# Which chunks of weights get their low parts from an accumulating DMA: fewer of them in four stages of a decoder trunk, and 18 feed-forward pairs by blocks

## The chip, the cores and the metric

The kernel runs on one core of one Trainium2 chip. The metric is the device time of one execution in microseconds (us). A profile is one further execution, recorded by the hardware profiler; it has a time of its own, and its span runs from the first to the last instruction. Engines are named as the profile names them: PE (TensorE's matmuls), PEld (its weight loads), DVE (VectorE), ACT (ScalarE), POOL (GpSimd) and SP (SyncE, which here issues transfers).

## The reference

Two layers over 512 tokens of width 1024, in float32. Cut to what matters here:

```python
for l in range(DEPTH):                                   # DEPTH = 2
    mod = c_act @ w_ada[l] + b_ada[l]                    # 6 x 1024 modulations
    sh1, sc1, g1, sh2, sc2, g2 = jnp.split(mod, 6, axis=-1)
    h = modulate(rmsnorm(x, norm1[l]), sh1, sc1)
    q, k, v, g_sw, p_in, gates = jnp.split(h @ w_in[l], IN_SPLITS, axis=-1)
    ...                                                  # rotary, chunked retention of 8 heads, pooling
    ret_d = (jax.nn.silu(g_sw) * ret) @ w_ret_o[l]
    pool_d = (pooled * pool_scale[l]) @ w_pool_o[l]
    a_ret, a_pool = jnp.split(gates, 2, axis=-1)
    merged = jax.nn.sigmoid(a_ret) * ret_d + jax.nn.sigmoid(a_pool) * pool_d
    x = x + g1[:, None, :] * (merged @ w_out[l])
    h2 = modulate(rmsnorm(x, norm2[l]), sh2, sc2)
    gate, up = jnp.split(h2 @ w_ffn_in[l], 2, axis=-1)   # 2 x 2816 columns
    x = x + g2[:, None, :] * ((jax.nn.silu(gate) * up) @ w_ffn_out[l])
return rmsnorm(x, final_norm)
```

## The kernel before, in words

**Numbers in two parts.** PE multiplies a shorter float format (float32r). To keep float32 accuracy, each operand is split into a high part, which is its float32r rounding, and a low part, which is the rest. A product is then three matmuls: high by high, low by high, high by low (`mm3`).

**Weights in chunks.** All weight blocks of 128 x 128 are packed on the host, in the order of use, into chunks of 8 blocks (128 x 1024, 512 KB). A layer takes 131 chunks. Within a layer, chunks 0 to 27 hold q, k, v, the output gate and the pooling input; 28 to 43 the sigmoid gate of the retention branch and its output projection in turn; 44 to 56 the pooling branch; 57 to 64 the output projection; 65 to 130 the feed-forward part. The gate and up projections come in 22 pairs of column tiles, two chunks each: pairs 0 to 10 are chunks 65 to 86, then 11 chunks of the down projection (87 to 97), then pairs 11 to 21 (98 to 119), then the rest of the down projection (120 to 130).

**Preparing a chunk.** `prep` loads a chunk into one of 3 `raw` tiles (a transfer on SP's queue) and writes the high part into one of 11 `w` tiles (`copy`, on DVE or ACT). The low part, in another `w` tile, is made in one of two ways. The local way subtracts the high part from the raw tile (`nc.either`: DVE or POOL). The added way lets ACT write the negated high part and lets a transfer issued by POOL read the same chunk again from memory and add it in (`accum_op=ALU.add`). Before the change every chunk from number 16 on takes the added way. An added chunk needs its raw tile only for the cast; a local chunk needs it until the subtraction has read it.

**Pairs by blocks.** Some pairs (the set `SEVEN`) are computed as four 2 x 2 blocks by a scheme of seven products, `seven`: 84 matmuls of 256 columns for a pair, where an ordinary pair takes 48 of 512. `seven_prep` loads the chunk, forms sums of blocks on DVE, and needs four `w` tiles for it. Before the change layer 0 has 9 such pairs (4, 6, ... 20) and layer 1 has 12 (two of every three from 4 on).

**Looking ahead.** `ahead` prepares the chunk in use and the next `LOOK` = 2. A chunk is known to belong to a pair by blocks only when that pair is reached, and by then `prep` has been called for it as for an ordinary chunk. Those chunks are loaded and prepared twice, and the first result is read by nothing.

**Modulations in the background.** `mod_tile` loads 512 KB of the modulation weights into a `raw` tile and reduces it on DVE. `background` issues the next one: two after each step of the two gate loops, one after each ordinary pair and after each step of the first down projection.

**The order of work.** All operations are recorded first. A planner (`Recorder`) gives each a due time, which it derives backwards from PE's order, then simulates the engines with a cost table and lists the instructions; each engine then works its list in that order. `LANDS` is the time that the planner allows for an accumulating transfer to land. Every instruction is emitted by one line, L409, so the profile's groups are told apart by tile names: `raw` and `w` as above, `h` the normalised input, `x` pair tiles (in the feed-forward part the sums of blocks), `r` rows kept in float32r, `t` temporaries, `ps` the PSUM banks.

Of the kernel before, what the change touches and what calls it, by code (L numbers as in the profile page):

```python
# [8 lines left out]
F32 = mybir.dt.float32  # L9
F32R = mybir.dt.float32r  # L10
AF = mybir.ActivationFunctionType
ALU = mybir.AluOpType
# [14 lines left out]
FT = FF // P  # L27
# [11 lines left out]
N_UNITS = DEPTH * (44 * KT + 8 * KT + 4 + 8 * 4 + 8 * KT + 2 * FT * KT + 8 * FT)  # L39
N_CHUNKS = -(-N_UNITS // UNITS) + DEPTH  # L40
LOOK = 2
ADD_SEVEN = False
FIRST_ADDED = 16


N_RAW, N_W, N_X, N_H, N_ROW, N_TEMP = 3, 11, 8, 2 * KT, 28, 9
# [4 lines left out]
STAT_TILES = {"out": 4, "ffn_out": 3}  # L51
STAT_AT = 2

SEVEN = [set(range(4, FT, 2)), {i for i in range(3, FT) if i % 3}]
HALF_KT = KT // 2


# [143 lines left out]

TABLES = (AF.Sigmoid, AF.Silu, AF.Abs_reciprocal_sqrt)
TABLE_US = 1.28
LANDS = 5.0
LATENCY = {"tensor": 0.19, "vector": 0.05, "scalar": 0.05, "gpsimd": 0.05, "sync": 1.6}


class Recorder:
# [32 lines left out]
    def deadlines(self):  # L241
# [13 lines left out]
        for op in reversed(self.ops):  # L255
# [3 lines left out]
            for o in op.after + reuse.get(op, []):  # L259
                if o.n > op.n:  # L260
                    op.due = min(op.due, o.due - LATENCY[e] - op.cost(e) - (LANDS if op.added else 0.0))
            if op.urgent and (e == "sync" or op.table is AF.Silu):
                op.due = op.n - 1e6

    def order(self):
# [48 lines left out]
        while len(out) < len(self.ops):  # L314
# [50 lines left out]
            if e == "scalar" and o.table is not None:  # L365
                end += TABLE_US * (o.table != table)
                table = o.table
            lands = LANDS if e == "gpsimd" and o.forms[e][0] == "dma_start" else 0.0
            if e == "tensor":
# [51 lines left out]
def trunk(ctx, tc, xT, cin, wada, vecs, wst, rot, trid, icnt, out):  # L421


    nc = Recorder()
# [5 lines left out]
    def ps():  # L430
        return nc.tile(pp, [P, S], F32, "ps", 8)

    def temp():
        return padded()[:, PAD:]
# [4 lines left out]
    def keep(dt=F32R):  # L439
        return nc.tile(ap, [P, S], dt, "r", N_ROW)  # L440

    def weights():
        return nc.tile(wp, [P, UNITS * P], F32R, "w", N_W)

    def raw_tile():
        return nc.tile(wp, [P, UNITS * P], F32, "raw", N_RAW)
# [45 lines left out]
    def prep(c, n=1):  # L492
        if c >= N_CHUNKS or c in his or c in sevens:
            return
        raw, hi, lo = raw_tile(), weights(), weights()
        nc.sync.dma_start(out=raw, in_=wst[c])
        if FIRST_ADDED <= c:

            copy(hi, raw)
            nc.scalar.activation(lo, hi.bitcast(F32), AF.Copy, scale=-1.0)  # L500
            nc.gpsimd.dma_start(out=lo, in_=wst[c], accum_op=ALU.add)
        else:
            w = UNITS * P // n
            for s_ in (slice(i * w, i * w + w) for i in range(n)):
                copy(hi[:, s_], raw[:, s_])
                nc.either.tensor_sub(out=lo[:, s_], in0=raw[:, s_], in1=hi[:, s_].bitcast(F32))
        his[c], los[c] = hi, lo
# [13 lines left out]
    def seven_prep(c):  # L521

        if sevens[c] is not None:
            return
        w = 2 * P
        af = raw_tile()
        nc.sync.dma_start(out=af, in_=wst[c])
        ah, al, sh, sl = (weights() for _ in range(4))
        a11, a12, a22, a21 = (af[:, n * w:n * w + w] for n in range(4))
        s34, s21 = keep(F32), keep(F32)  # L530
        nc.vector.tensor_sub(out=s34[:, :w], in0=a21, in1=a11)
        nc.vector.tensor_add(out=s21[:, :w], in0=s34[:, :w], in1=a22)
        nc.vector.tensor_add(out=s21[:, w:], in0=a21, in1=a22)
        nc.vector.tensor_sub(out=s34[:, w:], in0=a12, in1=s21[:, :w])
        copy(ah[:, :3 * w], af[:, :3 * w])
        if ADD_SEVEN:
            nc.scalar.activation(al[:, :3 * w], ah[:, :3 * w].bitcast(F32), AF.Copy, scale=-1.0)
            nc.gpsimd.dma_start(out=al[:, :3 * w], in_=wst[c][:, :3 * w], accum_op=ALU.add)
        else:
            nc.either.tensor_sub(out=al[:, :3 * w], in0=af[:, :3 * w], in1=ah[:, :3 * w].bitcast(F32))  # L540
        for n, sf in enumerate((s34, s21)):
            part = slice(n * S, n * S + S)
            copy(sh[:, part], sf)
            nc.either.tensor_sub(out=sl[:, part], in0=sf, in1=sh[:, part].bitcast(F32))
        sevens[c] = (ah, al), (sh, sl)
# [11 lines left out]
    def ahead(c):  # L557
        for cc in range(c, c + look[0] + 1):
            if cc in sevens:
                seven_prep(cc)  # L560
            else:
                prep(cc)
# [7 lines left out]
    def copy(out, src):  # L570
        nc.add({"scalar": ("copy", (), dict(out=out, in_=src)), "vector": ("tensor_copy", (), dict(out=out, in_=src))})
# [10 lines left out]
    def project(o, l, name, col, src, sl=FULL, k0=0, mid=None):  # L582
        n = len(src)
        for k in range(n):
            if mid and k == n // 2:
                mid()
            mm3(o[:, sl], unit(l, name, k0 + k, col), hs(src[k], sl), k == 0, k == n - 1)
# [13 lines left out]
    def mod_tile(l, t):  # L601

        w = raw_tile()
        nc.sync.dma_start(out=w, in_=wada[l, t])
        nc.vector.scalar_tensor_tensor(
            out=w, in0=w, scalar=1.0, in1=cact, op0=ALU.mult, op1=ALU.mult, accum_out=mods[l][:, t:t + 1],
        )
# [18 lines left out]
    def background(n=1):  # L626
        for _ in range(n):
            if waiting:
                mod_tile(*waiting.pop(0))
# [129 lines left out]
    def start(cols):  # L759

        ss = first_norm()
        o = [ps() for _ in cols]
        for k in range(KT):
            mod_tile(0, 8 + k)
            mod_tile(0, k)
            mod_bias(0, k, 1)
            mod_bias(0, 8 + k, 1)
            gain(0, 1, k, 1)
            prep(k, 2 if k == 0 else 1)
            for sl in (A, B) if k == 0 else (FULL,):  # L770
                if k == 0:
                    rstd(rs[:, sl], dict(ss)[sl], D)
                make_h(0, 1, k, sl, h[k])
            nc.urgent = False
            if k + 1 == KT:
                look[0] = LOOK
            for sl in (A, B) if k == 0 else (FULL,):
                for n, (a, b) in enumerate(((0, 0), (1, 0), (0, 1))):
                    for t, c in zip(o, cols):
                        nc.tensor.matmul(t[:, sl], lhsT=unit(0, "in", k, c)[a], rhs=h[k][b][:, sl],  # L780
                                         start=k + n == 0 and sl.start != S // 2, stop=k + n == KT + 1)
        nc.sync.dma_start(out=ic, in_=icnt)
        nc.sync.dma_start(out=tri, in_=trid)
        return dict(zip(cols, o))
# [65 lines left out]
    for l in range(DEPTH):  # L850
# [18 lines left out]
        def filler(mid=None):  # L869

            kind, n = fill.pop(0)
            if kind == "gate":
                gate(n)
            else:
                p0[n] = pool_in(tile_of(C_P + n * P, mid))
                pd[n] = pool_diff(n, p0.pop(n))
# [10 lines left out]
        for g in range(2):  # L887
# [33 lines left out]
            for i in range(4):  # L921
# [4 lines left out]
                for j in range(4):  # L926
                    c0 = min(j, 2) * P
                    w = S - c0
# [43 lines left out]
        for j in range(KT):  # L972
            o = ps()
            project(o, l, "in", C_A + j * P, h, mid=head_norm)
            sg = temp()
            nc.scalar.activation(sg, o, AF.Sigmoid)
            while fill:
                filler()
            rp = ps()
            project(rp, l, "ret_o", j * P, y)  # L980
            m = keep(F32)
            nc.vector.tensor_mul(out=m, in0=rp, in1=sg)
            m_.append(m)
            background(2)


        merged = []
# [85 lines left out]
        for f, (i0, i1) in enumerate(zip(FF_CUTS, FF_CUTS[1:])):  # L1073
            hid = []
            for i in range(i0, i1):
                if i in SEVEN[l]:
                    hid.append(seven(i))
# [114 lines left out]
```

## Time and profile before

| what | value |
|---|---|
| three runs | 1628.1 us median (1627.85 to 1629.76) |
| profiled execution, its own time | 1639.41 us |
| its span | 1637.6 us |
| PE busy | 1536.2 us (94%) |
| DVE, ACT, POOL busy | 980.3, 700.5, 337.1 us (60%, 43%, 21%) |
| mean granted clock of PE | 0.969 of full speed |
| transfers | 353.94 MB, 216 GB/s over the span |

A busy time is the union of an engine's instructions; a matmul that waits inside a stream shows as idle time ahead of the next one. PEclk is the clock granted to PE as a share of full speed. In a group's row the count stands behind an x, then the busy time, the mean duration of one in ns, and the idle time of the engine just before them with what ended it.

### The profile page before, as it was taken

The page shows a single profiled execution, that of the slowest core. Times are in us where ns is not written, and L with a number is a line of the kernel's source. Part 1 is how long each engine was busy: PE and PEld are TensorE (multiplying, and loading weights), DVE is VectorE, ACT ScalarE, POOL GpSimd, SP SyncE. Part 2 cuts the span into 40 slices and gives each one's busy share as a digit, 9 for nine tenths or more (in the row PEclk, how much of TensorE's full clock was granted, in tenths as well). Part 3 has the DMA queues.
Part 4 walks back from the last instruction along what each step waited for, and adds up shares of the span by engine and source line. Part 5 has one row for each costly group of instructions (what it writes and reads, how often), then busy time and mean ns, then how long its engine had stood idle before and what let it go on. Part 6 is the DMA issues. An engine that isn't in the chain of part 4 may idle for free.

```text
span 1637.6 us, 21319 instructions
## 1 busy us (share of the span) xinstructions
PE 1536.2 (94%) x8058; PEld 1314.2 (80%) x8058; DVE 980.3 (60%) x1748; ACT 700.5 (43%) x983; POOL 337.1 (21%) x370
## 2 busy tenths in 40 slices
PE   7999999799998899889999999999999899987897
PEld 6788878587987778788898887887888788887787
DVE  7887663455675645575266757535537784366733
ACT  2477542323553322333257766213237543244432
POOL 0033231121132111112111322211213322122211
PEclk9999999899999999899999999999999999999999
DMA  7758779999679799979977866999978789788893
GB/s 240 267 145 216 153 193 256 267 253 270 146 220 239 212 260 243 241 218 251 250 172 170 210 155 151 260 263 276 266 158 208 183 234 259 178 210 219 223 220 89
DMA packets 101225, 353.94 MB, mean 216 GB/s; under 512 B 11265, under 2 KB 13569, under 8 KB 101122
## 3 DMA queue, kind: packets, MB, share of 16 engines
q0 software_dynamic: 35568, 129.51, 42.9%
q1 hardware_dynamic: 65554, 223.07, 39.5%
q8 instruction: 63, 1.03, 0.2%
q14 instruction: 40, 0.33, 0.1%
HBM read 350.44 MB, written 2.10 MB: 215 GB/s over the span
## 4 chain that ended last, share of the span: by engine, by line
PE 43%; DMA 33%; DVE 11%; issue 8%; ACT 3%; POOL 1%; DVEq 0%; SPq 0%; ACTq 0%; POOLq 0%
PE ps L409 43%; DMA raw<-wada 13%; DMA w<-wst 10%; DMA raw<-wst 9%; DVE w L409 4%; DVE t L409 3%; ACT w L409 2%; DVE raw L409 2%; DVE r L409 1%; POOL w L409 1%; ACT t L409 1%; DMA xall<-xT 0%; POOL r L409 0%; DVE x L409 0%; DVE h L409 0%
## 5 line engine op out<-in xcount | busy, mean ns | idle before, releaser
L409 PE MATMUL ps<-h,w 128*128 128x512 f32 (+1 forms) x3828 | 791.9, 365 | 59.1 <-DMA w<-wst 51.3
L409 PEld LDWEIGHTS ps<-h,w 128*128 128x128 f32 x3828 | 655.9, 194 | 178.7 <-DMA w<-wst 56.0
L409 PE MATMUL ps<-r,w 128*128 128x512 f32 (+1 forms) x2430 | 484.5, 359 | 19.9 <-DVE r L409 17.6
L409 PEld LDWEIGHTS ps<-r,w 128*128 128x128 f32 x2430 | 405.1, 189 | 93.0 <-DVE r L409 20.9
L409 ACT ACTIVATE w<-w 128x1024 fp32r<-128x1024 f32 x247 | 260.3, 1058 | 426.3 <-DVE w L409 158.1
L409 POOL DMA_DIRECT2D w<-wst x247 | 220.3, 895 | 1052.4 <-ACT w L409 909.2
L409 DVE CAST w<-raw 128x1024 fp32r<-128x1024 f32 (+2 forms) x202 | 140.1, 693 | 200.7 <-DMA raw<-wst 134.1
L409 DVE SCALAR_TENSOR_TENSOR raw<-raw,cact 128x1024 f32<-128x1024 f32 x96 | 120.5, 1258 | 166.8 <-DMA raw<-wada 163.1
L409 ACT CAST w<-raw 128x1024 fp32r<-128x1024 f32 (+2 forms) x104 | 103.6, 997 | 161.8 <-DMA raw<-wst 126.7
L409 PE MATMUL ps<-x,w 128*128 128x256 f32 x1008 | 125.1, 279 | 1.0 <-ACT t L409 1.0
L409 PEld LDWEIGHTS ps<-x,w 128*128 128x128 f32 x1008 | 121.1, 188 | 1.2 <-ACT t L409 1.2
L409 PE MATMUL ps<-w,h 128*128 128x512 f32 x384 | 90.2, 395 | 0.0
L409 PEld LDWEIGHTS ps<-w,h 128*128 128x128 f32 x384 | 72.1, 188 | 17.5
L409 DVE TENSOR_TENSOR w<-raw,w 128x768 fp32r<-128x768 f32 (+2 forms) x55 | 64.4, 1172 | 24.7 <-DMA w<-wst 12.2
L409 DVE SCALAR_TENSOR_TENSOR xall<-ps,mod,xall 128x512 f32<-128x512 f32 (+1 forms) x62 | 38.8, 628 | 65.7 <-PE ps L409 65.6
L409 ACT CAST r<-t 128x512 fp32r<-128x512 f32 (+1 forms) x97 | 59.6, 617 | 34.4 <-DVE t L409 27.0
L409 DVE TENSOR_TENSOR w<-r,w 128x512 fp32r<-128x512 f32 x81 | 54.4, 688 | 24.8 <-ACT w L409 16.1
L409 DVE TENSOR_TENSOR t<-ps,t 128x512 f32<-128x512 f32 x81 | 55.3, 683 | 15.3 <-PE ps L409 13.2
L409 ACT CAST w<-r 128x512 fp32r<-128x512 f32 x55 | 32.5, 617 | 71.9 <-DVE r L409 40.7
L409 DVE TENSOR_TENSOR r<-raw 128x256 f32<-128x256 f32 x84 | 41.3, 514 | 35.1 <-DMA raw<-wst 34.9
L409 DVE TENSOR_TENSOR r<-t,r 128x512 fp32r<-128x512 f32 (+1 forms) x78 | 56.7, 727 | 7.4 <-ACT r L409 6.2
L409 ACT COPY t<-ps 32x512 f32<-32x512 f32 (+2 forms) x93 | 48.8, 527 | 18.9 <-DVE t L409 11.2
(95 smaller groups left out, 1005.1 us busy)
## 6 DMA issues: line engine op xcount, KB each, us to landing
raw<-wst SPq DMA_DIRECT2D x305, 512.0 KB, 5.9
w<-wst POOLq DMA_DIRECT2D x247, 512.0 KB, 8.3
raw<-wada SPq DMA_DIRECT2D x96, 512.0 KB, 5.7
x<-rot SPq DMA_DIRECT2D x32, 256.0 KB, 7.3
xall<-xT SPq DMA_DIRECT2D x4, 512.0 KB, 6.8
out<-t SPq DMA_DIRECT2D x7, 256.0 KB, 2.3
out<-t SPq DMA_DIRECT2D x2, 128.0 KB, 1.8
tri<-trid SPq DMA_DIRECT2D x1, 128.0 KB
```

The lines of the kernel that those rows point to most:

```text
L409: getattr(eng, method)(*[real(a) for a in args], **{k: real(v) for k, v in kw.items()})
```

## The change

The flag for all chunks from 16 on becomes a function of the chunk's place in its layer. Chunks 0 to 27 (in layer 0 from 16 on, as before) and 57 to 74 keep the added way. In chunks 28 to 56 (gates), 87 to 97 and 120 to 130 (the down projection, called the output stage in the change) only even numbers keep it. In chunks 75 to 86 and 98 to 119 (pairs 5 to 10 and 11 to 21) none does. Layer 1 now has the same 9 pairs by blocks as layer 0, 18 in all in place of 21. The loop over the first gate issues one modulation a step in place of two; those left over are issued by later calls of `background`. The planner's `LANDS` goes from 5.0 to 6.0. An unused flag and its branch in `seven_prep` are gone.

```diff
-ADD_SEVEN = False
 FIRST_ADDED = 16
+LAYER_CHUNKS = 131
+
+HALF_ADDED, NONE_ADDED = ((28, 57), (87, 98), (120, 131)), ((75, 87), (98, 120))
+
+
+def is_added(c):
+
+    n = c % LAYER_CHUNKS
+    if c < FIRST_ADDED or any(a <= n < b for a, b in NONE_ADDED):
+        return False
+    return n % 2 == 0 or not any(a <= n < b for a, b in HALF_ADDED)
...
-SEVEN = [set(range(4, FT, 2)), {i for i in range(3, FT) if i % 3}]
+SEVEN = [set(range(4, FT, 2)), set(range(4, FT, 2))]
...
-LANDS = 5.0
+LANDS = 6.0
...
-        if FIRST_ADDED <= c:
+        if is_added(c):
 
             copy(hi, raw)
             nc.scalar.activation(lo, hi.bitcast(F32), AF.Copy, scale=-1.0)
...
-        if ADD_SEVEN:
-            nc.scalar.activation(al[:, :3 * w], ah[:, :3 * w].bitcast(F32), AF.Copy, scale=-1.0)
-            nc.gpsimd.dma_start(out=al[:, :3 * w], in_=wst[c][:, :3 * w], accum_op=ALU.add)
-        else:
-            nc.either.tensor_sub(out=al[:, :3 * w], in0=af[:, :3 * w], in1=ah[:, :3 * w].bitcast(F32))
+        nc.either.tensor_sub(out=al[:, :3 * w], in0=af[:, :3 * w], in1=ah[:, :3 * w].bitcast(F32))
...
             m_.append(m)
-            background(2)
+            background()
```

## The prediction

> **What bounds the kernel now.** I read the page first: transfers and instruction groups.
>
> ```profile
> span 1637.6 us, 21319 instructions
> PE 1536.2 (94%) x8058; PEld 1314.2 (80%) x8058; DVE 980.3 (60%) x1748; ACT 700.5 (43%) x983; POOL 337.1 (21%) x370
> q0 software_dynamic: 35568, 129.51, 42.9%
> q1 hardware_dynamic: 65554, 223.07, 39.5%
> raw<-wst SPq DMA_DIRECT2D x305, 512.0 KB, 5.9
> w<-wst POOLq DMA_DIRECT2D x247, 512.0 KB, 8.3
> raw<-wada SPq DMA_DIRECT2D x96, 512.0 KB, 5.7
> ```
>
> PE is nearly full, so a saving must come from its idle 101 us or its clock. The two queues are not alike: the accumulating one takes 42.9% of the span, 702.5 us, for 247 chunks, so 2.84 us of all sixteen engines each. The plain one takes 646.9 us for 223.07 MB, so 1.52 us for a chunk of 0.524 MB. And 305 plain loads are 263 chunks plus 42: the chunks of all 21 pairs by blocks are loaded twice, and 247 = 263 - 16 says that the useless copies get accumulating transfers too.
>
> Next, PE's waits, then its timeline at some of them. A timeline row gives start, length, matmuls, and in brackets the idle time ahead.
>
> ```profile
> PE ps L409 <- DMA w<-wst: 53.5, 15, 8.8
> PE ps L409 <- DVE r L409: 18.0, 6, 8.5
> ...
> 247.29 5.66 PE L409 MATMUL ps<-h,w 128*128 128x512 f32 x24
> 252.79 5.66 PE L409 MATMUL ps<-r,w 128*128 128x512 f32 x24
> 312.06 3.35 PE L409 MATMUL ps<-r,w 128*128 128x512 f32 x7 [8.52 <-DVE r L409]
> ...
> 686.98 15.25 PE L409 MATMUL ps<-h,w 128*128 128x512 f32 x59 [2.65 <-DMA w<-wst]
> ...
> 736.75 14.29 PE L409 MATMUL ps<-h,w 128*128 128x512 f32 x59 [4.89 <-DMA w<-wst]
> 761.77 11.03 PE L409 MATMUL ps<-h,w 128*128 128x512 f32 x47 [2.35 <-DMA w<-wst]
> ...
> 1455.62 2.99 PE L409 MATMUL ps<-x,w 128*128 128x256 f32 x24
> 1460.57 2.99 PE L409 MATMUL ps<-x,w 128*128 128x256 f32 x24
> ```
>
> Of 101 us idle, 53.5 are waits for accumulated low parts. The typical place is the row at 736.75: a pair by blocks has ended, and the first ordinary chunk (512 columns) waits for its low part. What that chunk went through stands on ACT and POOL:
>
> ```profile
> 722.53 1.06 ACT L409 CAST w<-raw 128x1024 fp32r<-128x1024 f32 x1 [2.09 <-DMA raw<-wst]
> 727.44 1.05 ACT L409 ACTIVATE w<-w 128x1024 fp32r<-128x1024 f32 x1
> 728.98 0.88 POOL L409 DMA_DIRECT2D w<-wst  x1 [13.87 <-DVE r L409]
> ```
>
> High part done at 723.6, negation at 728.5, transfer issued at 729.9, landed at 736.75, when PE had waited since 731.9. A subtraction of 1.2 us after the cast would have been done before PE came.
>
> Third, the windows by stage: pairs 5 to 10, the down projection behind them and pairs 11 to 21 of layer 0; both sets of pairs of layer 1; the gates of layer 0, then of layer 1 in two pieces; three short ones at stalls; and the busiest stretch of DVE. The columns: start and end, length, busy time and count of PE, PEld, DVE, ACT and POOL, then the granted clock, DMA share and GB/s.
>
> ```profile
> 494.00:571.00 77.00, 66.86 (x395) 59.20 (x395) 50.73 (x96) 27.55 (x38) 13.56 (x15) 0.91 0.83 223
> 571.00:637.00 66.00, 63.75 (x269) 51.38 (x269) 25.51 (x44) 12.94 (x13) 9.88 (x12) 0.97 0.97 257
> 637.00:773.00 136.00, 122.74 (x710) 107.89 (x709) 88.66 (x167) 48.75 (x65) 22.45 (x28) 0.94 0.88 235
> 1291.60:1367.50 75.90, 66.24 (x432) 60.65 (x432) 57.99 (x99) 37.67 (x50) 23.00 (x21) 0.93 0.89 235
> 1428.00:1565.70 137.70, 118.84 (x782) 108.67 (x781) 92.32 (x161) 61.23 (x85) 31.60 (x31) 0.95 0.86 219
> 225.00:399.00 174.00, 161.06 (x681) 130.61 (x682) 80.38 (x133) 47.68 (x56) 32.24 (x34) 0.96 0.95 261
> 1012.00:1121.00 109.00, 105.43 (x461) 86.18 (x459) 50.00 (x84) 29.35 (x38) 21.80 (x30) 0.99 0.95 259
> 1121.00:1200.00 79.00, 78.65 (x333) 64.28 (x334) 43.20 (x72) 25.67 (x31) 16.18 (x17) 0.96 0.99 258
> 686.00:693.00 7.00, 6.02 (x14) 4.76 (x15) 2.95 (x6) 0.00 (x0) 0.72 (x1) 0.52 1.06 272
> 734.00:741.00 7.00, 4.25 (x10) 3.41 (x11) 3.36 (x6) 1.06 (x1) 0.86 (x1) 0.51 1.06 266
> 761.00:766.00 5.00, 4.23 (x18) 3.49 (x19) 2.41 (x4) 1.06 (x1) 0.62 (x1) 1.00 1.05 224
> ...
> 50.00:100.00 50.00, 49.62 (x217) 39.92 (x216) 41.88 (x67) 31.22 (x48) 4.16 (x2) 1.00 0.57 195
> ```
>
> A stall costs more than its idle time: behind it the granted clock falls to a half for some 3 to 7 us (0.52 and 0.51). After the shorter gap at 761.77 (2.35 us) it stayed at 1.00.
>
> Transfers explain the pairs. One ordinary pair and one by blocks take seven plain loads (two each, two useless, one modulation) and four accumulating ones: 7 x 1.52 + 4 x 2.84 = 22.0 us. PE needs 11.0 for the ordinary pair (24 matmuls each 5.50, from 247.29 to 252.79) and 9.9 for the other (a chunk every 4.95, from 1455.62 to 1460.57), 20.9 together. Transfers are the longer, before any latency. The stages last 77 + 136 + 75.9 + 137.7 = 426.6 us for 34 pairs, 25.1 for two; 22.0 of 25.1 is the 0.88 in the third window's DMA column.
>
> **The change, part by part.**
>
> *Three pairs fewer by blocks.* 11.0 - 9.9 = 1.1 us of PE each, 3.3 in all. PE's floor for the 34 pairs becomes 18 x 11.0 + 16 x 9.9 = 356.4 us.
>
> *No accumulating transfer in these pairs.* Removed per two pairs: four transfers, four negations on ACT, four issues on POOL. Added: four subtractions. Transfers fall to 7 x 1.52 = 10.6 us of 20.9. The costs of the rest:
>
> ```profile
> L409 ACT ACTIVATE w<-w 128x1024 fp32r<-128x1024 f32 x247 | 260.3, 1058 | 426.3 <-DVE w L409 158.1 <-PE ps L409 129.1 <-issue 125.7
> L409 DVE TENSOR_TENSOR w<-raw,w 128x1024 fp32r<-128x1024 f32 x13 | 15.9, 1223 | 3.2 <-ACT w L409 2.8
> L409 POOL TENSOR_TENSOR w<-raw,w 128x1024 fp32r<-128x1024 f32 x2 | 4.8, 2425 | 5.4 <-ACT w L409 5.4
> L409 DVE CAST w<-raw 128x1024 fp32r<-128x1024 f32 x18 | 12.5, 694 | 2.5 <-DMA raw<-wst 2.5
> L409 DVE CAST w<-r 128x512 fp32r<-128x512 f32 x12 | 5.1, 428 | 1.0 <-DMA w<-wst 0.4
> L409 DVE CAST w<-raw 128x768 fp32r<-128x768 f32 x5 | 2.8, 556 | 5.2 <-DMA raw<-wst 5.2
> L409 DVE TENSOR_TENSOR w<-raw,w 128x768 fp32r<-128x768 f32 x10 | 9.5, 955 | 3.3 <-ACT w L409 2.9
> L409 DVE TENSOR_TENSOR r<-raw 128x256 f32<-128x256 f32 x20 | 7.8, 420 | 11.9 <-DMA raw<-wst 11.8
> ```
>
> The last five rows are from pairs 11 to 21 of layer 0 alone. DVE is busy 88.7 us there; 22 subtractions of 1.22 add 26.9, so 115.6 against a PE floor of 6 x 11.0 + 5 x 9.9 = 115.5. That is full. But 12.5 + 5.1 + 2.8 = 20.4 us of it are casts that ACT may do, and ACT loses some 24 negations of 1.06. With them on ACT, DVE has 95 us of 115.5, 82%, and ACT about 55. The cover for the subtractions is thus DVE's free 18%; without it each costs up to 1.22 us. I take them as mostly hidden.
>
> What is late next is the raw tile. There are three, and a local chunk holds one through cast and subtraction. Held per two pairs, from issue: four ordinary chunks 5.9 + 0.9 + 1.2 = 8.0, two by blocks 5.9 + 3.2 (four 256-wide operations of 0.42, cast 0.56, subtraction 0.96) = 9.1, one modulation 7.0. That is 57.2 us of tile time, 19.1 over three tiles, plus 2.33 us for each us that a load waits for its reader. I take a wait of 1 us (about one operation ahead of it in the queue): 21.4 a period. From below it is 20.9, PE's own; from above, the rivals. 17 x 21.4 = 364, and I leave 9 us for four stalls of 2 to 3 us with their clock: 373. Against 426.6 the gain is 53.6.
>
> By the Trainium skill (TensorE: Matmul & The Clock Gate, Part 1: The HAM clock gate) the clock drops after an idle window of about 3.4 us. By that rule the four stalls left in would cost idle time only, and the result would be some 4 us lower. The trace does not agree in full: the row at 686.98, behind 2.65 us idle, shows 0.52.
>
> *Half of them in the gates.* Before, a step of the first gate loop has 4 plain and 2 accumulating transfers, 11.8 us for 11.0 of PE; of the second, 3.5 plain and 1.5 accumulating, 9.6 for 8.24 (36 matmuls). After, with one modulation in the first loop, 3 and 1, 7.4; and 3.5 and 0.75, 7.5. Both fit again. Layer 0 loses 12.9 idle and 0.04 x 161 for the clock, 19.4; layer 1 3.9 and 4.2, 8.1; together 27.5. The 8.52 us at 312.06, at the change from one loop to the other, is a wait for DVE, whose queue stands behind a late modulation. I take 21 of 27.5, since the second loop still uses 91% of the transfers' time.
>
> *The down projections.* In layer 0, 66 us against 11 chunks x 5.5 = 60.5. Half the accumulating transfers go; I take 3 of 5.5.
>
> *Modulations moved, LANDS, the dead branch.* Eight modulations of each layer move to a later call; the count of 96 stays. In layer 1 they fall into pairs that had none; the seven loads above include one per two pairs. Their cost is DVE's 1.3 us each, inside its free share, and 10 us in all if that is gone. LANDS only sets how early the planner lists the accumulating issues: 0, between -5 and +5. The branch was not used: 0.
>
> **Sum.** 53.6 + 21 + 3 = 77.6 (the 3.3 are in the 373). The profiled execution took 1639.4: 1561.8. The median of the runs shown is 1628.1, 0.9931 of that, so **1551 us**. With every loss gone it would be 426.6 - 356.4 + 27.5 + 5.5 = 103.2 less, 1536, which is 1526.
>
> **The rivals.**
>
> *VectorE becomes the bound.* For it: 115.6 us of work against 115.5, if the casts stay on DVE. Its busiest 50 us stretch is 41.88, 84%. At that rate the four stages take 115.6/0.84 = 138; (50.7 + 14.7)/0.84 = 78; layer 1, where each pair by blocks that is dropped saves DVE at least eight operations of 0.42 and two of 0.96, 5.3 us, and three modulations come in at the first set, (58.0 - 5.3 + 14.7 + 4.0)/0.84 = 85 and (92.3 - 10.6 + 26.9)/0.84 = 129. Sum 430 for 426.6; with 24 from gates and down projection 1619, times 0.9931 **1608**. Against it: casts can move, and ACT is at 36% in the third window. By the Trainium skill (SBUF — State Buffer, Who interferes with whom) a DVE instruction with two SBUF inputs and a GpSimd instruction that reads SBUF exclude each other, so POOL would be no relief. No number above counts on POOL.
>
> *The change doesn't do what it says: the stall stays, by another name.* The wait at the ordinary chunk is really for `w` tiles that the blocks hold, and the transfer's latency was hidden behind it. Then only gates and down projection gain, 24, less 3.3: 1618.7, **1608**. Against it: the cast at 722.53 had its tile nine us before PE came.
>
> *Slower: the raw tiles.* If a load waits w us for its reader, a period is (57.2 + 7w)/3. From w = 3.2 it is over 26.5, and the 17 periods eat the 24 gained elsewhere; at 4 us it is 28.4, 483 us, 32 slower net: 1671, **1660**. For it: DVE works in order and would be fuller. Against it: loads land sooner when transfers are at half load.
>
> **How the numbers follow.** Forecast 0.67, VectorE 0.2, stall under another name 0.06, raw tiles 0.07. The range runs from 1524, the floor, to 1610, past the VectorE case and the stall's. Faster by over 0.2%, about what a measurement of this kernel can tell: 0.90; same 0.03; slower 0.07.
>
> **What would show it.** Right: waits of PE for w<-wst under 15 us; the windows of the pairs at 21 to 22 us for two; w<-wst near 129 issues (56 and 72 by the ranges, one empty chunk); DMA share there near 0.5; clock at 0.99; no wait of 8 us at the gates. Wrong: PE waiting for DVE w at the ordinary chunks, DVE above 90% (VectorE), or DVE and ACT idle on raw<-wst in the pairs (raw tiles).

## The result and the profile after

The changed kernel takes 1553.64 us, the median of four runs (1550.0 to 1557.65), against 1627.97 us (1626.12 to 1629.76) for the kernel before on the same chip. The ratio is 0.9544, with a 95% interval of 0.9518 to 0.9570. The profiled execution took 1553.07 us.

The page of the changed kernel, to be held against the first fence of the prediction:

```profile
span 1551.3 us, 20752 instructions
PE 1507.6 (97%) x7950; PEld 1290.2 (83%) x7950; DVE 1022.4 (66%) x1677; ACT 669.8 (43%) x949; POOL 292.2 (19%) x279
q1 hardware_dynamic: 64690, 219.92, 42.6%
q0 software_dynamic: 18576, 67.64, 24.3%
raw<-wst SPq DMA_DIRECT2D x299, 512.0 KB, 4.6
w<-wst POOLq DMA_DIRECT2D x129, 512.0 KB, 7.6
raw<-wada SPq DMA_DIRECT2D x96, 512.0 KB, 4.9
```

PE's idle time fell from 101 us to 44. Accumulating transfers are 129, as counted from the ranges. A plain chunk now lands in 4.6 us, not 5.9; an accumulating one still needs 7.6.

PE's waits, the longest first, and the one that used to lead:

```profile
PE ps L421 <- DVE r L421: 5.1, 4, 2.7
PE ps L421 <- DVE w L421: 4.6, 5, 1.6
...
PE ps L421 <- DMA w<-wst: 1.4, 1, 1.4
```

The 53.5 us behind accumulated low parts are 1.4. No wait of PE is over 4 us. Now the windows of the same stages: pairs 5 to 10, the down projection behind them and pairs 11 to 21 of layer 0, both sets of pairs of layer 1, and the gates of layer 0 (columns as in the prediction).

```profile
484.00:547.20 63.20, 62.18 (x402) 56.05 (x400) 54.38 (x85) 26.03 (x37) 20.64 (x12) 1.00 0.52 165
547.20:612.00 64.80, 62.15 (x267) 50.55 (x266) 35.43 (x51) 12.40 (x13) 5.86 (x5) 0.97 0.78 230
612.00:725.40 113.40, 113.40 (x709) 101.58 (x708) 99.41 (x158) 40.25 (x54) 24.26 (x16) 1.00 0.56 178
1235.30:1301.90 66.60, 63.85 (x399) 56.84 (x398) 58.14 (x84) 27.16 (x39) 17.84 (x12) 1.00 0.49 159
1364.00:1479.50 115.50, 115.50 (x710) 103.58 (x709) 85.40 (x132) 48.28 (x66) 9.77 (x7) 1.00 0.49 154
218.00:386.00 168.00, 164.71 (x711) 134.21 (x710) 89.34 (x131) 48.57 (x60) 25.01 (x28) 0.99 0.79 219
```

In pairs 11 to 21 of both layers PE is busy all the time at full clock: 113.4 and 115.5 us where there were 136 and 137.7. The four sets of pairs together take 358.7 us in place of 426.6. VectorE is the fuller for it, 99.4 of 113.4 us, 88%, and the transfers are at half load.

PE's timeline, cut at the points where its operands change (first matmul of pair 4, first and last of a down projection), divides both profiled executions into stages. Layer 1 begins where layer 0 ends.

| stage, us | before | after |
|---|---|---|
| layer 0 up to pair 4 | 485.0 | 474.2 |
| pairs 4 to 10 | 86.1 | 73.0 |
| down projection, first part | 65.5 | 64.7 |
| pairs 11 to 21 | 135.9 | 113.5 |
| down projection, second part | 61.4 | 61.6 |
| layer 1 up to pair 4 | 448.8 | 437.4 |
| pairs 4 to 10 | 84.6 | 77.4 |
| down projection, first part | 60.4 | 62.1 |
| pairs 11 to 21 | 137.7 | 115.5 |

The pairs give 64.9 us, the two stretches that hold the gates 22.2, and the down projections nothing. These figures compare one execution of each kernel, and that of before was 11 us above its median, that of after at its own; in which stages those 11 us lie no run tells.

### The profile page after: what moved, and what is told of

It is laid out like the page before. It is cut to its first block, busy times and chain, and to the rows that moved or that the text cites. A ratio compares the mean times of both kernels' runs of the same rounds, so it can differ in the third digit from the quotient of the medians.

```text
span 1551.3 us, 20752 instructions
## 1 busy us (share of the span) xinstructions
PE 1507.6 (97%) x7950; PEld 1290.2 (83%) x7950; DVE 1022.4 (66%) x1677; ACT 669.8 (43%) x949; POOL 292.2 (19%) x279
## 5 line engine op out<-in xcount | busy, mean ns | idle before, releaser
L421 ACT CAST w<-raw 128x1024 fp32r<-128x1024 f32 (+2 forms) x192 | 194.5, 1014 | 350.9 <-DMA raw<-wst 228.0
L421 POOL DMA_DIRECT2D w<-wst x129 | 115.4, 894 | 734.9 <-ACT w L421 673.4
L421 DVE TENSOR_TENSOR w<-raw,w 128x1024 fp32r<-128x1024 f32 (+2 forms) x158 | 194.2, 1234 | 88.5 <-PE ps L421 45.1
L421 ACT ACTIVATE w<-w 128x1024 fp32r<-128x1024 f32 x129 | 136.6, 1059 | 176.9 <-PE ps L421 60.8
L421 DVE CAST w<-raw 128x1024 fp32r<-128x1024 f32 (+2 forms) x108 | 77.4, 717 | 106.3 <-DMA raw<-wst 58.7
L421 PE MATMUL ps<-x,w 128*128 128x256 f32 x864 | 109.3, 281 | 8.0 <-DVE w L421 4.2
L421 PEld LDWEIGHTS ps<-x,w 128*128 128x128 f32 x864 | 104.5, 190 | 9.6 <-DVE w L421 5.1
L421 POOL TENSOR_TENSOR r<-t,r 128x512 fp32r<-128x512 f32 x41 | 67.5, 1655 | 157.5 <-ACT r L421 144.9
L421 DVE SCALAR_TENSOR_TENSOR xall<-ps,mod,xall 128x512 f32<-128x512 f32 (+1 forms) x62 | 38.7, 629 | 65.9 <-PE ps L421 65.8
L421 ACT ACTIVATE t<-ps 128x512 f32<-128x512 f32 x74 | 43.7, 592 | 50.4 <-PE ps L421 50.3
L421 ACT ACTIVATE t<-xall 128x256 f32<-128x256 f32 (+1 forms) x46 | 22.3, 497 | 82.3 <-DVE xall L421 79.1
L421 ACT COPY t<-ps 32x512 f32<-32x512 f32 (+2 forms) x90 | 48.0, 535 | 21.4 <-DVE t L421 11.9
```

Source lines behind the costliest of these rows:

```text
L421: getattr(eng, method)(*[real(a) for a in args], **{k: real(v) for k, v in kw.items()})
```

## The experiments

All times are medians against the kernel before, run on the same chip. Chips differ by some us (the kernel before had medians of 1628 to 1634), so kernels are compared by their ratios.

| kernel | us | ratio to before, 95% |
|---|---|---|
| the change | 1553.6 | 0.9544 (0.9518 to 0.9570) |
| pairs alone | 1565.8 | 0.9603 (0.9556 to 0.9651) |
| gates and down projections alone | 1621.5 | 0.9932 (0.9908 to 0.9956) |
| before, no useless preparations | 1553.9 | 0.9517 (0.9482 to 0.9553) |
| before, useless ones local | 1587.6 | 0.9712 (0.9684 to 0.9740) |
| before, ordinary ones local | 1575.7 | 0.9637 (0.9598 to 0.9676) |
| before, useless transfers without tiles | 1675.1 | 1.0213 (1.0153 to 1.0274) |
| change, casts on VectorE | 1568.8 | 0.9605 (0.9563 to 0.9648) |
| change, two raw tiles | 1646.8 | 1.0071 (1.0045 to 1.0096) |
| change, 21 pairs by blocks | 1561.4 | 0.9537 (0.9499 to 0.9574) |
| change, two modulations a step | 1551.4 | 0.9475 (0.9429 to 0.9521) |
| change, no useless preparations | 1539.4 | 0.9419 (0.9380 to 0.9458) |
| the same with 24 pairs by blocks | 1532.0 | 0.9358 (0.9327 to 0.9390) |

### The two halves of the change

The pairs alone, on the kernel before (`is_added` is the changed kernel's function with the other range empty):

```diff
+NONE_ADDED, HALF_ADDED = ((75, 87), (98, 120)), ()
...
-        if FIRST_ADDED <= c:
+        if is_added(c):
```

> The kernel before, with only the pairs 5 to 10 and 11 to 21 made local; 21 pairs by blocks, two modulations a step and the accumulating transfers elsewhere as before. If the pairs carry the gain as the sum has it (53.6 of 77.6) and more as the changed kernel's trace has it (about 68): 1555 to 1575 us. If VectorE is the bound where two of three pairs go by blocks (92.3 + 26.9 = 119 us of work for 113 of PE in layer 1): 1580 to 1600 us.

The gates and down projections alone:

```diff
+NONE_ADDED, HALF_ADDED = (), ((28, 57), (87, 98), (120, 131))
...
-        if FIRST_ADDED <= c:
+        if is_added(c):
...
             m_.append(m)
-            background(2)
+            background()
```

> The kernel before, with only the gates and the down projections at every other chunk, and one modulation a step in the first gate loop; the pairs as before. By the sum 24 us: 1600 to 1608 us, with the 8.5 us wait between the gate loops gone and the stalls in the pairs as they were. If the gain of the change lies wholly in the pairs: 1620 to 1630 us.

The pairs alone bring 4.0%, nearly all of the 4.6%. The gates alone bring 0.7%, 11 to 12 us, half of the 24 expected; 1621.5 us lies in the range given for a gain wholly in the pairs, on a chip where the kernel before took 1634.0. In the two profiled executions layer 0 reaches pair 4 at 472.7 us in place of 485.0, and layer 1 needs 439.4 up to its pair 4 in place of 448.8: 21.7 us, as the sum had it. Layer 0 gains nearly 7 us more in pairs 4 to 10 and the down projection behind them. In layer 1 the same stages give 9.6 us back: the pairs go from 84.6 to 88.8, the down projection from 60.4 to 65.8. Those pairs still wait for low parts, and they now also get the modulations that the gates passed on; how much of the 9.6 us these cost was not tested. So the two profiles differ by 20.9 us, and most of what is missing in the medians comes from the 11 us by which the profiled execution of before stood above its median. In all, PE still waits 53 us for low parts:

```profile
PE ps L420 <- DMA w<-wst: 53.3, 20, 7.5
```

So the gates' share is less certain than the pairs': 21.7 us by the profiles' stages, 11 to 12 by the medians.

### Is it the time of the transfers, or the latency of each?

The prediction gave two reasons for the stalls in one breath: the transfers need 22.0 us for each 20.9 of PE, and an accumulated low part comes some 8 us after its negation. The first kernel takes the useless preparations out and leaves every other chunk accumulating:

```diff
+def by_blocks(c):
+    l, n = divmod(c, 131)
+    if 65 <= n < 87:
+        return (n - 65) // 2 in SEVEN[l]
+    return 98 <= n < 120 and 11 + (n - 98) // 2 in SEVEN[l]
...
-        if c >= N_CHUNKS or c in his or c in sevens:
+        if c >= N_CHUNKS or c in his or c in sevens or by_blocks(c):
```

> The kernel before, with the useless preparation of the 42 chunks by blocks left out (their first plain load, cast, negation and accumulating transfer); all low parts of the other chunks from 16 on still come from accumulating transfers, 205 in place of 247. Theory A, the transfers' time: two pairs need 5 x 1.52 + 2 x 2.84 = 13.3 us of the transfers in place of 22.0, under PE's 20.9, so the stalls at the ordinary chunks go nearly as they did with the change: 1565 to 1580 us. Theory B, the latency of each accumulating transfer: it still lands some 7 to 8 us after its negation, so most of the stalls of 3 to 5 us stay, only the gates' queue is unchanged: 1600 to 1625 us, PE waits on DMA w<-wst over 30 us.

It gains as much as the whole change, and is faster than either theory had it (1565 us at best), although the wait at the gates is still there with 8.9 us. Its accumulating transfers on the page, PE's waits for them, and the windows of its pairs 11 to 21 (layer 0, layer 1):

```profile
w<-wst POOLq DMA_DIRECT2D x205, 512.0 KB, 7.8
```

```profile
PE ps L418 <- DMA w<-wst: 3.1, 3, 1.9
```

```profile
615.60:731.00 115.40, 115.40 (x709) 103.55 (x708) 77.66 (x138) 43.15 (x60) 20.67 (x22) 1.00 0.68 184
1366.90:1480.10 113.20, 113.20 (x781) 105.31 (x780) 85.79 (x135) 49.14 (x73) 31.91 (x27) 1.00 0.58 155
```

An accumulating transfer still takes 7.8 us to land, and PE hardly waits. A latency of 8 us alone is thus no stall; it has to meet something else.

The next two kernels keep all preparations and make half of the transfers in the pairs local, once the useless half and once the ordinary half. Both need 16.3 us of the transfers for two pairs in turn.

```diff
# useless ones local
-        if FIRST_ADDED <= c:
+        if FIRST_ADDED <= c and (not 75 <= c % 131 < 120 or 87 <= c % 131 < 98 or not by_blocks(c)):
# ordinary ones local
-        if FIRST_ADDED <= c:
+        if FIRST_ADDED <= c and (not 75 <= c % 131 < 120 or 87 <= c % 131 < 98 or by_blocks(c)):
```

> The kernel before; in pairs 5 to 10 and 11 to 21 the useless preparations are local, the ordinary chunks keep the accumulating transfers. Two pairs need 7 x 1.52 + 2 x 2.84 = 16.3 us of the transfers. Theory A, the transfers' time: under 20.9, so the stalls go, 1555 to 1575 us. Theory B, the latency of the ordinary chunk's own transfer: the stalls stay, 1600 to 1630 us.

> The mirror of the last: in those pairs the ordinary chunks are local, the useless preparations keep the accumulating transfers; the same 16.3 us of transfers for two pairs, and the same number of subtractions for VectorE but in layer 1, where fewer chunks are ordinary. Theory A: the same time as the last kernel within 10 us, 1555 to 1575. Theory B: much faster than the last, by 30 us and more.

Windows of pairs 11 to 21 of layer 0 and pairs 4 to 10 of layer 1, the useless ones local in the first fence, the ordinary ones local in the second:

```profile
621.90:737.30 115.40, 115.40 (x709) 103.52 (x708) 92.07 (x159) 44.55 (x59) 26.26 (x24) 1.00 0.78 226
1247.60:1332.30 84.70, 76.61 (x507) 70.39 (x506) 65.89 (x104) 42.87 (x60) 25.53 (x20) 0.92 0.57 166
```

```profile
623.40:736.90 113.50, 113.50 (x710) 101.67 (x708) 88.64 (x149) 51.36 (x68) 26.41 (x25) 1.00 0.78 222
1243.10:1314.00 70.90, 70.30 (x505) 66.14 (x505) 65.30 (x102) 38.34 (x53) 21.49 (x19) 1.00 0.83 221
```

Neither theory fits as a whole: the times lie 12 us apart, both above theory A's range, and not the 30 us and more of theory B. In pairs 11 to 21 of layer 0, where pairs by blocks and ordinary ones alternate, both free PE entirely. Raw tiles, casts and useless loads are all still there, so these were not the cause; halving the accumulating transfers, whichever half, is enough there. That is what the sum of 22.0 against 20.9 says, though the transfers were busy for 0.88 of that stage before and not throughout. In the first set of layer 1, where two pairs by blocks follow each other, the two kernels part. With the useless ones local it stays at 84.7 us, what it was before, at a transfer share of only 0.57; with the ordinary ones local it takes 70.9 at 0.83, with VectorE as busy in both (65.9 and 65.3 us). There the latency of the ordinary chunk's own transfer decides. In pairs 11 to 21 of layer 1 both gain again: 121.5 and 116.1 us in place of 137.7. One stall of the first set, on ACT, POOL and PE, with the useless ones local:

```profile
1297.63 1.05 ACT L418 CAST w<-raw 128x1024 fp32r<-128x1024 f32 x1 [1.20 <-DMA raw<-wst]
1298.72 1.06 ACT L418 ACTIVATE w<-w 128x1024 fp32r<-128x1024 f32 x1
...
1300.14 0.88 POOL L418 DMA_DIRECT2D w<-wst  x1 [9.26 <-DVE r L418]
...
1309.32 14.63 PE L418 MATMUL ps<-h,w 128*128 128x512 f32 x59 [4.58 <-DMA w<-wst]
```

The cast waits for its load until 1297.6, the transfer is issued at 1300.1 and lands at 1309.3, and PE was there at 1304.7. Ahead of that load stand those of the blocks and of their useless copies. Without the useless copies, in the first kernel, the same pairs take 70.0 us with their ordinary chunks still accumulating. On this evidence it takes both, a late load and the 8 to 9 us of the transfer.

A last kernel was to put the transfers back without the tiles:

```diff
+        if by_blocks(c):
+            dumped.add(c)
+            near = his[max(his)].bitcast(F32)
+            for n in range(2):
+                part = slice(n * S, n * S + S)
+                nc.scalar.copy(out=rs[:, :1], in_=near[:, :1])
+                nc.sync.dma_start(out=rs, in_=wst[c][:, part])
+                nc.scalar.activation(acc, near[:, part], AF.Copy, scale=-1.0)
+                nc.gpsimd.dma_start(out=acc, in_=wst[c][:, part], accum_op=ALU.add)
+            return
```

> The kernel before without the useless preparations, but with their transfers: for each of the 42 chunks the same bytes are loaded plainly and again accumulating, in halves, into two tiles that hold nothing at that time; the negation on ACT is kept, the cast and the hold of a raw tile and of two w tiles are not. Theory A, the time of the transfers (22.0 us for two pairs against 20.9 of PE): the stalls at the ordinary chunks come back, 1610 to 1635 us. Theory C, the tiles that the useless preparations held: they don't, 1553 to 1575 us.

The stalls came back and more, 1675 us, but the run decides less than it seems to. ScalarE's own waits in it:

```profile
ACT rs L418 <- DMA rs<-wst: 209.6, 67, 8.6
...
ACT acc L418 <- DMA acc<-wst: 143.4, 44, 11.0
```

ScalarE works its list in order, and stood 353 us behind the halves that were to land before the next could start. Casts and negations of real chunks stood behind it. So the run shows a cost from above and does not separate the transfers' time from the w tiles, which an accumulating transfer holds some 8 us longer; in both half-and-half kernels the two went down together.

The waits of the engines that write the w tiles tell more. ACT's and DVE's waits for a w tile in pairs 11 to 21 of layer 0, first of the kernel before, then of the one without the useless preparations:

```profile
ACT w L409 <- PE ps L409: 6.9, 1, 6.9
ACT w L409 <- DMA w<-wst: 4.6, 1, 4.6
...
ACT w L418 <- PE ps L418: 26.8, 16, 3.3
DVE w L418 <- PE ps L418: 10.6, 10, 4.4
```

They come to 11.9 us before, with 0.4 of DVE, and to 37.4 without the useless preparations, where PE is busy throughout; with the useless ones local they are 12.1, with the ordinary ones 10.7. The stalls went and these waits did not, so a lack of w tiles is not what made the stalls there. What did fall is the time of a load into a raw tile: in that window the median lands in 6.5 us before, in 4.1 without the useless preparations, and in 4.6 and 4.9 in the half-and-half kernels. In pairs 11 to 21 of layer 1 ACT and DVE waited 46.9 us for tiles in which an accumulating transfer had still to land. What those waits cost PE there stays open.

### VectorE as the bound

```diff
-                copy(hi[:, s_], raw[:, s_])
+                (nc.vector.tensor_copy(out=hi[:, s_], in_=raw[:, s_]) if c >= FIRST_ADDED else copy(hi[:, s_], raw[:, s_]))
...
-        copy(ah[:, :3 * w], af[:, :3 * w])
+        nc.vector.tensor_copy(out=ah[:, :3 * w], in_=af[:, :3 * w])
...
-            copy(sh[:, part], sf)
+            nc.vector.tensor_copy(out=sh[:, part], in_=sf)
```

> The changed kernel with the casts of local chunks and of the blocks' weights on VectorE alone, so that ScalarE can't take them. VectorE has 99.4 us of work in the 113.4 of pairs 11 to 21 of layer 0; 20 casts of 0.69 and 8 of 0.56 make it 118. If VectorE can't run fuller than 84%, as the rival has it: 140 there, and about 1615 us in all. If it can run nearly full: the stage takes 118 to 122, and all 1560 to 1570 us. If its work has nothing to do with it: 1550 to 1557.

Pairs 11 to 21 of layer 0 with the casts on VectorE:

```profile
616.30:735.90 119.60, 117.28 (x709) 103.55 (x708) 107.02 (x173) 16.43 (x28) 21.26 (x16) 1.00 0.50 154
```

119.6 us, VectorE busy 107.0 of them, 89%, and not the 118 us of work expected. The ratio is 0.9605 against 0.9544, and the intervals only just touch. VectorE can run fuller than the 84% of the rival. PE does begin to wait for it once ScalarE doesn't share the casts: its waits for DVE w are 12.3 us in all, against 4.6 in the changed kernel.

### The raw tiles

```diff
-N_RAW, N_W, N_X, N_H, N_ROW, N_TEMP = 3, 11, 8, 2 * KT, 28, 9
+N_RAW, N_W, N_X, N_H, N_ROW, N_TEMP = 2, 11, 8, 2 * KT, 28, 9
```

> The changed kernel with two raw tiles in place of three. By the prediction's formula with the landing times of the changed profile (4.6 and 4.9 us) two pairs hold the tiles 49 us and 7 us more for each us a load waits: with three tiles 16 to 19 us, under PE's 20.5; with two 24 to 28, which is 60 to 125 us more over the pairs alone: 1615 to 1700. If raw tiles are far from the bound: under 1580.

1646.8 us, 0.7% slower than before the change. Pairs 11 to 21 of layer 0, then of layer 1:

```profile
652.70:785.00 132.30, 121.09 (x709) 105.51 (x709) 100.94 (x156) 39.46 (x60) 22.93 (x18) 0.99 0.51 163
1453.60:1567.10 113.50, 113.50 (x709) 101.69 (x708) 87.96 (x143) 36.27 (x49) 17.43 (x12) 1.00 0.47 146
```

Layer 0 has seven loads for two pairs; its 132.3 us are 5.5 periods of 24.1. Loads land in 4.3 us in this run, those of the modulations in 4.0, and with these the prediction's formula holds the tiles for 45.9 us, 23.0 over two tiles at w = 0; the 24.1 are reached with w = 0.3. In layer 1 no modulation is loaded there any more: 40.6 us over two tiles, 20.3; measured is 20.6, with PE busy throughout. So the formula fits both sets with almost no waiting time, and with three tiles and loads landing in 4.6 us the need is 16 us for 20.5 of PE. The loss is not all in the pairs, as was expected: against the changed kernel they lose 40 us, and the two stretches up to pair 4 lose 43.

### Single parts of the change, undone

```diff
# 21 pairs by blocks
-SEVEN = [set(range(4, FT, 2)), set(range(4, FT, 2))]
+SEVEN = [set(range(4, FT, 2)), {i for i in range(3, FT) if i % 3}]
# two modulations a step
             m_.append(m)
-            background()
+            background(2)
```

> The changed kernel with the 21 pairs by blocks of before (12 in layer 1). PE has 3.3 us less to do. If PE is the bound in the pairs of layer 1 (115.5 us for pairs 11 to 21): 1547 to 1552 us. If VectorE is full there with two of three pairs by blocks (85.4 + 2 x 5.3 and more of 113, with seven pairs in a row of two): 1555 to 1575, with PE waiting for DVE w in layer 1.

> The changed kernel with two modulations a step in the first gate loop, as before. The first loop then needs 4 x 1.52 + 2.84 = 8.9 us of the transfers in 11.0 of PE, which still fits. If the accumulating transfers made the wait at the gates: no change within 5 us, 1549 to 1558. If the modulations did (VectorE's queue standing behind them): the wait of 8.5 us comes back, 1562 to 1572.

With 21 pairs by blocks the ratio is 0.9537 against 0.9544: no difference that these runs can tell. PE has 3.3 us less to do, and in layer 1 it loses about as much or more: in the profiled execution, 7 us above the median of its kernel, the first set of pairs there takes 85.8 us in place of 77.4, and PE's waits for VectorE are 16.9 us in all.

```profile
PE ps L421 <- DVE w L421: 16.9, 13, 4.9
```

With two modulations a step the ratio is 0.9475 (0.9429 to 0.9521): not slower, perhaps somewhat faster. The 8.5 us wait at the gates did not come back; its place has a wait of 1.04 us. With the pairs alone changed, the gates with all their accumulating transfers and two modulations, it was still 6.76 us. With the gates and down projections alone changed, one modulation a step and `LANDS` at 5.0 as before, no wait stands there. So neither the two modulations nor `LANDS` decides; what the kernels without that wait have in common is that half of the accumulating transfers in the gates are gone. Undoing `LANDS` alone was not tested.

### Without the useless preparations

The guard `by_blocks` from above, on the changed kernel; then also two of every three pairs by blocks from the fifth on in both layers.

> The changed kernel, with the useless preparation of the 36 chunks by blocks left out. It takes 36 plain loads, 36 casts and 36 subtractions out. If VectorE or the raw tiles still hold PE up in the pairs, PE's waits there (about 7 us) and behind them go: 1542 to 1548 us. If PE's own work is the bound after the change, nothing moves: 1550 to 1557 us.

```diff
-SEVEN = [set(range(4, FT, 2)), set(range(4, FT, 2))]
+SEVEN = [{i for i in range(3, FT) if i % 3}, {i for i in range(3, FT) if i % 3}]
```

> The changed kernel without the useless preparations and with two of every three pairs by blocks from the fifth on in both layers, 24 in place of 18. PE has 6 x 1.1 to 1.4 us less to do: with VectorE's work small enough 1530 to 1534 us, against 1539 for the kernel with 18. If VectorE is full (per three pairs two by blocks, without useless preparations about 2 x 12.9 + 5.2 of 30.8): 1540 to 1560.

Both are faster than the change: 0.9419 and 0.9358. The first, 1539.4 us, is faster than either expectation had it. Pairs 4 to 10 go from 73.0 and 77.4 us to 69.7 and 70.4 with the guard, 10.3 of the 13.4 us by which the spans differ. With 24 pairs by blocks pairs 11 to 21 take 110.6 us in both layers, with PE busy throughout:

```profile
600.60:711.20 110.60, 110.60 (x781) 102.71 (x781) 94.44 (x151) 42.60 (x65) 27.48 (x22) 1.00 0.42 135
1344.30:1454.90 110.60, 110.60 (x781) 102.70 (x780) 89.26 (x140) 46.11 (x69) 22.35 (x17) 1.00 0.41 129
```

Without the useless subtractions VectorE has room for more pairs by blocks. This version takes 1532 us, as expected with VectorE's work small enough.

## Why the prediction was right, and where it was off

**The time.** 1551 was forecast and 1553.6 measured. Some of that is luck: two errors that cancel. The two spans differ by 86.3 us, not by 77.6; but the profiled execution of before was 11 us above its median, that of after was at its median, so that the step from the profile to the median (0.9931, 10.8 us) did not apply to the result. Against the medians the gain is 74.3 us, against 77.1 forecast.

**The pairs: right in the mechanism, the remainder mis-sized.** Forecast 373 us for the four sets, measured 358.7; the floor with PE alone was put at 356.4, with a pair by blocks at 9.9 us. In layer 0 such a pair now takes 9.5, which is why pairs 11 to 21 there lie below their floor of 115.5 (the two issue rates below). The stalls at the ordinary chunks went as the sum of transfers had it, and the share of the transfers fell to about 0.5 as foretold. The step that failed is "what is late next is the raw tile", with a landing of 5.9 us and a wait of 1 us for each load, 21.4 us a period. Loads land in 4.6 us once the transfers are at half load, and the kernel with two tiles shows almost no waiting. The period is 20.6 to 21.0 in pairs 11 to 21, PE's own. The 9 us for four stalls were too many: in pairs 5 to 10 about 4 us of idle time is left, in pairs 11 to 21 none.

**Two causes told as one.** The prediction read a single stall, at 736.75 us, as late by the transfer's latency, and the stage as bound by the transfers' time. In pairs 11 to 21 of layer 0 fewer transfers are enough; in the first set of layer 1 the half-and-half kernels show the latency as well. The reading of that stall also left out a part. The negation at 727.44 came nearly 4 us after the cast had ended. ACT's list had this row ahead of it, which waited for VectorE:

```profile
726.91 0.64 ACT L409 ACTIVATE t<-t 128x512 f32<-128x512 f32 x1 [2.82 <-DVE t L409]
```

So of the 4.89 us that PE waited, nearly 4 may be due to the order of ACT's list, and not to the transfer. No run tested that alone. The prediction also named the 42 useless preparations only in passing. They are the cheaper end to pull: leaving them out gains as much as the whole change.

**The subtractions.** Forecast: hidden, with the casts on ScalarE, VectorE at 82% and ScalarE at about 55 us. Measured in that window: 88%, and 40 us. The casts from raw tiles did move (20 of the 1024 wide ones on ScalarE there, 1 on VectorE). The casts of the sums of blocks, of which the prediction moved VectorE's 5.1 us to ScalarE as well, did not: VectorE has 19 of them, 8.5 us, more than the 4 us by which its 99.4 us exceed the 95 forecast. The subtractions cost 25.0 us in place of 26.9: 18 in the window and not 22, but each longer:

```profile
L421 DVE CAST w<-r 128x512 fp32r<-128x512 f32 x19 | 8.5, 448 | 0.9
L421 DVE TENSOR_TENSOR w<-raw,w 128x1024 fp32r<-128x1024 f32 x18 | 25.0, 1392 | 5.0 <-ACT w L421 4.1 <-issue 0.9
L421 ACT CAST w<-raw 128x1024 fp32r<-128x1024 f32 x20 | 21.1, 1054 | 41.4 <-DMA raw<-wst 18.0 <-PE ps L421 16.5 <-DVE w L421 6.8
```

A subtraction took 1.39 us in place of 1.22. The Trainium skill (SBUF — State Buffer, Who interferes with whom) has it that a VectorE instruction with two SBUF inputs and a GpSimd instruction that reads SBUF shut each other out. The changed kernel's trace agrees, on POOL and on DVE:

```profile
657.67 2.08 POOL L421 TENSOR_TENSOR w<-raw,w 128x768 fp32r<-128x768 f32 x1 [4.33 <-ACT w L421]
...
657.96 2.08 DVE L421 TENSOR_TENSOR r<-raw,r 128x256 f32<-128x256 f32 x1
```

An operation that takes VectorE 0.42 us alone took 2.08 us beside one of POOL, and both end within 0.3 us of each other. POOL's help thus costs VectorE time, as the rival had it, but with room enough that PE, busy throughout this window, did not see it.

**Three pairs fewer by blocks** was put down as 3.3 us of PE and no more. The kernel with 21 pairs is not faster: VectorE gives the 3.3 back. The cost was right for PE and wrong for the path, at least in the first set of layer 1.

**The gates** were sized right by the profiles: 21 forecast, 22.2 measured up to pair 4 of both layers; by the medians of the kernel with gates and down projections alone it is half of that. The reason given for the wait at 312.06, a queue behind a late modulation, is half the story; the two modulations a step can stay if the accumulating transfers are halved.

**The down projections**: 3 forecast, about -1 measured (65.5 to 64.7 in layer 0, 60.4 to 62.1 in layer 1). The term failed: halving the accumulating transfers was not what they needed. With all of them in place and only the useless preparations gone, the first down projection of layer 0 takes 60.4 us, PE's own, at a transfer share of 0.97. In the changed kernel the stall at its start only changed its name, from a transfer to VectorE:

```profile
556.89 3.42 PE L421 MATMUL ps<-r,w 128*128 128x512 f32 x8 [2.65 <-DVE r L421]
```

**The rivals.** VectorE as the bound: not at 84%, as the kernel with all casts on it shows. The stall by another name: no, PE idles 4.6 us for DVE w in place of 53.5. Raw tiles: the mechanism is real, and comes in with one tile fewer. The 1 us that a load was to wait for its reader was too much: 0.3 us fit the kernel with two tiles.

## What to carry to other kernels

Price transfers by the time they take on the transfer engines, per kind, and set the sum of a stage against the bounding engine in that stage; a latency can be hidden as long as what starts it comes early, a sum that is longer than the period can't. Look for work that is prepared and then read by nothing: here a count of loads against chunks showed it, and dropping it was worth as much as re-balancing the rest. When a term of the gain rests on other loads shrinking too, take the landing times of an unloaded stretch, not those of the loaded one.

## What the runs showed of the hardware that had not been expected

**Two issue rates at one clock.** The same 709 or 710 matmuls of pairs 11 to 21 took 113.5 us in layer 0 and 115.5 in layer 1 of the changed kernel, busy throughout at a granted clock of 1.00. The difference lies in those of 256 columns: two chunks by blocks follow each other after 4.76 us in the one and 4.95 in the other, as PE's timeline has it. What sets the rate was not found.

```profile
624.24 2.88 PE L421 MATMUL ps<-x,w 128*128 128x256 f32 x24
...
629.00 2.88 PE L421 MATMUL ps<-x,w 128*128 128x256 f32 x24
...
1418.20 2.99 PE L421 MATMUL ps<-x,w 128*128 128x256 f32 x24
...
1423.15 2.99 PE L421 MATMUL ps<-x,w 128*128 128x256 f32 x24
```

**Half clock after short gaps.** Windows of the changed kernel behind gaps of 2.02, 2.96, 2.65 and 1.95 us:

```profile
426.70:430.00 3.30, 3.30 (x16) 3.17 (x15) 2.36 (x7) 2.57 (x4) 0.82 (x1) 0.50 0.00 1
474.50:477.80 3.30, 3.30 (x17) 3.30 (x17) 3.30 (x6) 2.40 (x5) 1.69 (x1) 0.50 0.00 0
556.50:559.70 3.20, 2.81 (x7) 2.18 (x8) 3.17 (x5) 0.00 (x0) 0.86 (x1) 0.50 0.94 225
792.60:796.00 3.40, 3.40 (x28) 3.35 (x29) 2.75 (x8) 0.47 (x1) 0.00 (x0) 1.00 1.05 276
```

2.02 us was enough at one place, and 1.95, or 2.35 in the kernel before, was not at others. The Trainium skill (TensorE: Matmul & The Clock Gate, Part 1: The HAM clock gate) speaks of an idle window of about 3.4 us; the gaps here are shorter. Whether the place of a gap against such windows decides was not tested.
